# A coarser projection step and a swapped order of two preparation streams in a planned one-core mixer kernel

## Chip, core and metric

The kernel runs on one core of a Trainium2 chip. The metric is device time in microseconds, the median of several executions. TensorE is called PE, VectorE DVE, ScalarE ACT, GpSimd POOL; SP issues most transfers. PE's clock has two levels, 2.4 GHz (1.0 in the profile's column of granted clock) and 1.2 GHz (0.5).

## What is computed

One layer over 640 tokens (128 of context, 512 latent) of width 1024. A normed and modulated input `h` is projected once to 8832 columns; two branches use them and are merged.

```
z = h @ w_in                                   # r,k,v,decay,iclr | gate A | q,k,v | gate B | merge gates
branch A: per head and direction, a scan over the tokens:
    sa = s @ a_t ;  s = s * w_t + sa b_t^T + v_t k_t^T ;  y_t = s @ r_t
branch B: windowed attention with cached context keys and a sink
out = x + gate * ((sig(m_a) * (yA*silu(g_a)) @ w_oA + sig(m_b) * (yB*silu(g_b)) @ w_oB) @ w_out)
```

## The kernel before, in words

All products with big weights are float32 made of three float32r products: weight high by input high, weight low by input high, weight high by input low (tiles `wh`, `wl` by `hh`, `hl`). A block of 128 columns is two halves of 320 tokens, a half is 8 slices (`k`) of 1024 inputs, so 24 products of 320 columns into one PSUM tile `g`. The generator `products` runs through the blocks. It also loads the weights (`wr`, three buffers, over SP), splits them (ACT makes `wh`, POOL makes `wl`) and lets the evacuation (`late`) of the half before come behind slices 0 and 2.

The scan of branch A is done in chunks of 64 tokens for 8 pairs of heads. Each pair passes through five streams, and each stream is a generator that stops wherever something has to become ready:

- `fronts`: key norm, decay and rate gates by a small product (`mi<-dw`, `mi<-da`, evacuated by ACT into `cs` and `ta`), the scaled operands `ar` and `bk`, the chunk matrices (four groups of 10 products `mi<-ar,bk 64x64`, each evacuated by DVE into `XT`), and the bonus (`mi<-rk`, evacuated by DVE into `rk`).
- `backs`: inversion of those matrices. DVE first inverts 16 by 16 corners (14 rounds of `X<-M`, `M<-M,X` between two transposes); then PE and ACT go through six stages of 32 by 32 products for each of two halves, from `mi<-ident,X` to `mi<-XT,X`.
- `all_items`: score matrices and transposed operands (`sc<-ar,bk`, `sc<-ident,rkv`, `sc<-ident,bk`).
- `chains`: the scan itself, 10 steps for each pair, one after the other. A step is `ur<-St` on PE, `U` on DVE, `st<-U,XT` on PE, `SB` on ACT, `st<-SB` on PE, the new state `St` on DVE.
- `finishes`: group norm of the result on DVE, its transposes (`sc<-ident,ytok`).

The order on PE, ACT, DVE and POOL is written by `deal`. It keeps an estimated time for each engine (`Clock`). Before each step of the projection it goes through the list of streams from the front, and the first one that may go on (its last results count as ready, its condition holds, DVE and ACT are not over 2 us behind) makes one step; then the list is gone through from the front again. When no stream may go on, the projection makes one step, up to its next `yield`. Engines execute in that order, so an instruction that is not ready holds up all that stands behind it on its engine. The projection consists of 3312 products in this part; when they are used up, what is left of the streams runs alone, with the 16 products of `gate_rows` (`g<-wg`) strewn in by the scheduler. Small PSUM tiles `mi` have two buffers and `sc` one, so the third group of `mi` waits for the evacuation of the first. After `deal` comes the attention, then the output products.

Of the kernel before, what the change touches and what calls it, by code (L numbers as in the profile page):

```python
# [170 lines left out]
def hybrid_step(ctx, tc, a):  # L171
# [12 lines left out]
    def T(shape, tag, bufs, dt=F32, name=None):  # L184
        bufs = NB.get(tag, bufs)
        return sb.tile(shape, dt, tag=tag, name=name or tag, bufs=bufs)

    def PG():
        return psp.tile([P, 512], F32, tag="g", name="g", bufs=2)
# [193 lines left out]
    def products(blocks):  # L383


        blocks = iter(blocks)
        todo, raws = [], []
        over = [False]

        def more_raw():  # L390
            while len(raws) < 3 and not over[0]:
                if not todo or todo[-1][1] == 2:
                    b = next(blocks, END)
                    if b is END:
                        over[0] = True
                    if b is END or b is None:
                        return
                    todo.append([b, 0, None, None])
                t = todo[-1]
                raw = T([P, 4, P], "wr", 3, name="wr")  # L400
                k = 4 * t[1]
                nc.sync.dma_start(out=raw, in_=t[0][0].rearrange("(k p) n -> p k n", p=P)[:, k:k + 4, t[0][1]:t[0][1] + P])
                t[1] += 1
                raws.append((t, k, raw))

        def split():
            if not raws:
                return
            t, k, raw = raws.pop(0)
            if k == 0:  # L410
                t[2] = T([P, KB, P], "wh", 2, F32R, name="wh")
                t[3] = T([P, KB, P], "wl", 2, F32R, name="wl")
            act.copy(out=t[2][:, k:k + 4], in_=raw)
            pool_e.tensor_tensor(out=t[3][:, k:k + 4], in0=raw, in1=t[2][:, k:k + 4].bitcast(F32), op=ALU.subtract)

        more_raw()
        late = None
        done = 0
        while not over[0] or todo:
            if not todo:  # L420
                yield IDLE
                more_raw()
                continue
            t = todo.pop(0)
            while any(r[0] is t for r in raws):
                split()
            if t[1] < 2:
                todo.insert(0, t)
                more_raw()
                todo.pop(0)  # L430
                while any(r[0] is t for r in raws):
                    split()
            more_raw()
            (w, c0, xh, xl, evac, more), _, wh, wl = t
            for half in range(2):
                ps = PG()
                o = ps[:, :HALF + more]
                s = slice(0, HALF + more) if half == 0 else slice(HALF - more, TOK)
                for k in range(KB):
                    pe.matmul(out=o, lhsT=wh[:, k, :], rhs=xh[k][:, s], start=(k == 0), stop=False)  # L440
                    pe.matmul(out=o, lhsT=wl[:, k, :], rhs=xh[k][:, s], start=False, stop=False)
                    pe.matmul(out=o, lhsT=wh[:, k, :], rhs=xl[k][:, s], start=False, stop=(k == KB - 1))
                    if k == 0 and late:
                        late = late[0](*late[1:])
                    if k == 2 and late:
                        late = late()
                    if k == 2:
                        split()
                        more_raw()
                    if k == KB - 1:  # L450
                        late = (evac, half, o, s)
                        if not todo and half == 1:
                            late = evac(half, o, s)
                            if late:
                                late()
                            late = None
                    yield None

    def gemm(*args, **kw):
        for _ in products([gemm_block(*args, **kw)]):  # L460
            pass
# [73 lines left out]
    def filler():  # L535

        for nm, col, nb, kind in (("kb", COL_KB, 2, "plain"), ("vb", COL_VB, 2, "plain"), ("q", COL_Q, 8, "plain"),
                                  ("ga", COL_GA, 8, "silu"),
                                  ("gb", COL_GB, 8, "silu"), ("ma", COL_MA, 8, "tanh"), ("mb", COL_MB, 8, "tanh")):
            for b in range(nb):  # L540
                spills[nm, b] = dram_.tile([P, TOK], F32, name="sp_%s%d" % (nm, b))
                yield spill(col + P * b, spills[nm, b], kind)
# [20 lines left out]
    for _ in products([conv_block(COL_WA, wa, 24)]):  # L563
        pass
# [15 lines left out]
    def project(i):  # L580

        us[i]["rkv"] = [dram_.tile([P, TOK], F32, name="sp_rkv%d%d" % (i, j)) for j in range(3)]
        return [conv_spill(c0 + P * i, us[i]["rkv"][j], 8 * j + i, i if j == 2 else None)
                for j, c0 in enumerate((COL_R, COL_K, COL_V))]
# [14 lines left out]
    def load(i):  # L599
        if i < NPAIR and us[i].get("projected") and "loaded" not in us[i]:  # L600
            us[i]["loaded"] = [T([P, TOK], "rkv", 4, name="rkv%d" % j) for j in range(3)]
            for t, d in zip(us[i]["loaded"], us[i]["rkv"]):
                nc.sync.dma_start(out=t, in_=d)
            us[i]["at"] = clock.at["pe"] + 5
# [857 lines left out]
    def plan():  # L1462

        fill = filler()
        nxt = 0
        while True:
            if nxt < NPAIR and (nxt < 2 or us[nxt - 2].get("begun")):
                yield from project(nxt)
                nxt += 1
                continue  # L1470
            b = next(fill, None)
            if b is None and nxt == NPAIR:
                return
            yield b

    def fronts():
        for i in range(NPAIR):
            yield lambda: us[i].get("projected")
            us[i]["begun"] = True
            load(i)  # L1480
            clock.run.ready = max(clock.run.ready, us[i]["at"])
            yield
            yield from front(i, us[i])

    def backs():
        for i in range(NPAIR):
            yield lambda: us[i].get("ready")
            yield from back(us[i])
            us[i]["prepared"] = True

    def all_items():
        for i in range(NPAIR):
            yield lambda: us[i].get("ready")
            for n in range(5):
                yield lambda: i == 0 or us[i - 1].get("step", 0) >= 2 * n + 2
                yield from items(us[i], n)
                us[i]["items"] = n + 1
            us[i]["itemized"] = True

    def chains():  # L1500
        for i in range(NPAIR):
            yield lambda: us[i].get("prepared") and us[i].get("items", 0) >= 1 and (i < 2 or us[i - 2].get("finished"))
            for x in chain(i, us[i]):
                yield x
                yield lambda: us[i]["items"] >= min(us[i]["step"] + 1, 9) // 2 + 1
            us[i]["chained"] = True

    def finishes():
        for i in range(NPAIR):
            yield lambda: us[i].get("chained")  # L1510
            yield from finish(i, us[i])
            us[i]["finished"] = True

    def deal(main, others):


        runs = [Run(o, clock) for o in others]
        more = True
        while more or any(r.steps for r in runs):
            went = True  # L1520
            while went:
                went = False
                for j, r in enumerate(runs):
                    if not r.open() or j and max(clock.at["dve"], clock.at["act"]) > clock.at["pe"] + BACKLOG:
                        continue
                    clock.run = r
                    r.step()
                    clock.run, went = None, True
                    break
            before = clock.at["pe"]  # L1530
            more = more and next(main, END) is not END
            if clock.at["pe"] == before:
                clock.at["pe"] += 0.1

    with tc.tile_pool(name="psc", bufs=1, space=PSUM) as pools["scan"], tc.manual_schedule(engines=ORDERED):
        deal(products(plan()), [chains(), finishes(), all_items(), backs(), fronts()])
    for _ in gate_rows():
        pass
    pools["ur"] = ctx.enter_context(tc.tile_pool(name="psu", bufs=1, space=PSUM))
# [87 lines left out]
```

## Time and profile before

| | us |
|---|---|
| median of 3 runs | 1523.27 |
| lowest, highest | 1522.05, 1525.69 |
| profiled execution | 1514.24 |
| its span (first to last instruction) | 1512.5 |

The profiled execution took 9.0 us less than the median of the runs. In the profile an fp32 product of the small kind is two records, a float32r product one. A bracket at the end of a line tells how long the engine had been idle before it and what ended that. "issue" stands where nothing that the profile shows was waited for.

### The profile page before, as it was taken

The page shows a single profiled execution, that of the slowest core. Times are in us where ns is not written, and L with a number is a line of the kernel's source. Part 1 is how long each engine was busy: PE and PEld are TensorE (multiplying, and loading weights), DVE is VectorE, ACT ScalarE, POOL GpSimd, SP SyncE. Part 2 cuts the span into 40 slices and gives each one's busy share as a digit, 9 for nine tenths or more (in the row PEclk, how much of TensorE's full clock was granted, in tenths as well). Part 3 has the DMA queues.
Part 4 walks back from the last instruction along what each step waited for, and adds up shares of the span by engine and source line. Part 5 has one row for each costly group of instructions (what it writes and reads, how often), then busy time and mean ns, then how long its engine had stood idle before and what let it go on. Part 6 is the DMA issues. An engine that isn't in the chain of part 4 may idle for free.

```text
span 1512.5 us, 40280 instructions
## 1 busy us (share of the span) xinstructions
PE 1326.8 (88%) x16959; PEld 1094.7 (72%) x16959; DVE 789.3 (52%) x1818; ACT 682.5 (45%) x1661; POOL 451.3 (30%) x476
## 2 busy tenths in 40 slices
PE   5699899989989989998999999999854589999996
PEld 0499788878878887787887887788443356668985
DVE  2437516804553582465357147236226898763636
ACT  2335264364346426534643652653433465654322
POOL 0323333323233322323223243242222222233630
PEclk9699899999999999999999999999965599999999
DMA  8143312322221232223122212223322242224532
GB/s 315 39 136 106 97 52 80 96 70 61 87 89 56 65 95 67 69 82 100 52 80 85 78 57 87 73 73 102 116 69 66 79 137 68 85 74 149 183 111 93
DMA packets 154419, 139.05 MB, mean 92 GB/s; under 512 B 16435, under 2 KB 130294, under 8 KB 154238
## 3 DMA queue, kind: packets, MB, share of 16 engines
q1 hardware_dynamic: 144328, 126.27, 26.9%
q10 hardware_dynamic: 9910, 10.21, 2.1%
q8 instruction: 133, 2.18, 0.6%
q14 instruction: 48, 0.39, 0.1%
HBM read 102.88 MB, written 33.56 MB: 90 GB/s over the span
## 4 chain that ended last, share of the span: by engine, by line
PE 67%; DVE 14%; ACT 7%; issue 5%; DMA 1%; POOL 1%; ACTq 0%; DVEq 0%; SPq 0%; POOLq 0%
PE g L139 38%; PE mi L139 10%; PE st L139 8%; PE sc L139 7%; PE ur L139 5%; DVE X L139 3%; DVE M L139 2%; ACT L139 1%; DVE ytok L139 1%; ACT X L139 1%; DVE St L139 1%; ACT SB L139 1%; DVE gnt L139 1%; DVE o L139 1%; DVE nm L139 1%
## 5 line engine op out<-in xcount | busy, mean ns | idle before, releaser
L139 POOL TENSOR_TENSOR wl<-wr,wh 128x512 fp32r<-128x512 f32 x170 | 230.3, 1357 | 694.9 <-ACT wh L139 658.0
L139 PE MATMUL g<-hh,wh 128*128 128x320 f32 (+1 forms) x1104 | 383.9, 348 | 9.8 <-DVE stg L139 4.9
L139 PE MATMUL g<-hl,wh 128*128 128x320 f32 (+1 forms) x1104 | 350.8, 318 | 1.5 <-POOL hl L139 1.2
L139 PE MATMUL g<-hh,wl 128*128 128x320 f32 (+1 forms) x1104 | 351.1, 318 | 0.8 <-issue 0.8
L139 PEld LDWEIGHTS g<-hh,wh 128*128 128x128 f32 x1104 | 215.2, 195 | 31.3 <-DVE stg L139 5.8
L139 PEld LDWEIGHTS g<-hh,wl 128*128 128x128 f32 x1104 | 216.8, 196 | 2.1 <-issue 1.1
L139 PEld LDWEIGHTS g<-hl,wh 128*128 128x128 f32 x1104 | 215.9, 196 | 3.0 <-POOL hl L139 2.2
L139 ACT CAST wh<-wr 128x512 fp32r<-128x512 f32 x170 | 104.5, 619 | 17.9 <-DMA wr<-in_w_oB 5.4
L139 ACT COPY SB<-st 64x128 f32<-64x128 f32 x160 | 41.8, 261 | 106.5 <-PE st L139 105.6
L139 ACT COPY U<-st 128x128 f32<-128x128 f32 x80 | 21.4, 267 | 145.1 <-DVE St L139 135.0
L139 DVE SCALAR_TENSOR_TENSOR stg<-g,vt,stg 128x127 f32<-128x127 f32 (+1 forms) x144 | 60.7, 436 | 38.3 <-ACT stg L139 35.6
L139 DVE SCALAR_TENSOR_TENSOR St<-St,pc,st 128x64 f32<-128x64 f32 x128 | 30.2, 276 | 93.5 <-PE st L139 85.3
L139 PE MATMUL mi<-ar,bk 64*64 64x64 f32 (+1 forms) x960 | 72.8, 247 | 6.3 <-DVE XT L139 6.0
L139 ACT COPY SB<-sc 64x256 f32<-64x256 f32 (+1 forms) x160 | 55.3, 372 | 47.8 <-PE sc L139 46.5
L139 DVE TENSOR_TENSOR S<-sc,smask 128x512 f32<-128x512 f32 x40 | 27.5, 687 | 90.8 <-PE mi L139 89.3
L139 POOL TENSOR_TENSOR S<-S,smask 128x512 f32<-128x512 f32 x40 | 49.1, 1227 | 79.9 <-ACT S L139 79.2
L139 DVE TENSOR_TENSOR U<-ur,U 128x128 f32<-128x128 f32 x72 | 20.8, 289 | 93.2 <-PE ur L139 90.2
L139 PEld LDWEIGHTS mi<-ar,bk 64*64 64x64 f32 (+1 forms) x960 | 62.2, 156 | 8.7 <-issue 4.5
L139 ACT ACTIVATE Pl<-ur,nm 128x384 f32<-128x384 f32 (+1 forms) x64 | 40.6, 636 | 34.5 <-DVE nm L139 27.6
L139 PE MATMUL ur<-KH,qt 128*128 128x512 f32 (+2 forms) x80 | 34.4, 434 | 22.7 <-ACT Pc L139 10.0
L139 ACT COPY X<-mi 32x320 f32<-32x320 f32 (+5 forms) x120 | 35.8, 330 | 39.0 <-PE mi L139 38.4
L139 ACT COPY PT<-sc 128x512 f32<-128x512 f32 x60 | 35.1, 585 | 39.9 <-PE sc L139 38.3
(284 smaller groups left out, 2934.2 us busy)
## 6 DMA issues: line engine op xcount, KB each, us to landing
wr<-in_w_in SPq DMA_DIRECT2D x138, 256.0 KB
sp_rkv<-stg SPq DMA_DIRECT2D x48, 160.0 KB
rkv<-sp_rkv SPq DMA_DIRECT2D x24, 320.0 KB
wa_t<-in_w_ada SPq DMA_DIRECT2D x11, 512.0 KB
wg<-in_w_ada SPq DMA_DIRECT2D x16, 256.0 KB
wr<-in_w_oA SPq DMA_DIRECT2D x16, 256.0 KB
wr<-in_w_oB SPq DMA_DIRECT2D x16, 256.0 KB
wo<-in_w_out SPq DMA_DIRECT2D x16, 256.0 KB
```

Of the source, the lines that this page charges most:

```text
L139: return f(**kw)
```

## The change

A step of the projection now ends behind every second slice, so six products go out between two looks at the streams, where it was three. And `fronts` stands ahead of `backs` in the list.

```
                     late = None
-                    yield None
+                    if k % 2:
+                        yield None
...
-        deal(products(plan()), [chains(), finishes(), all_items(), backs(), fronts()])
+        deal(products(plan()), [chains(), finishes(), all_items(), fronts(), backs()])
```

Neither line adds or removes arithmetic; they move instructions on every engine between the first front and the last chain. From the last `sc<-ident,ytok` on, the order on PE, ACT, DVE and POOL is the same in both.

First place, PE, the chunk matrices of the seventh pair (`mi<-ar,bk 64x64`, 40 products in four groups) among the steps of the chain of the pair before. Before:

```order
L139 MATMUL g<-hl,wh 128x320
L139 MATMUL mi<-ar,bk 64x64 x30
L139 MATMUL ur<-St_375,ar 64x64 x8
L139 MATMUL mi<-ar,bk 64x64 x10
L139 MATMUL g<-hh,wh 128x320
L139 MATMUL g<-hh,wl 128x320
L139 MATMUL g<-hl,wh 128x320
L139 MATMUL st<-U,XT 64x64 x4
```

Now:

```order
L139 MATMUL g<-hl,wh 128x320
L139 MATMUL st<-U,XT 64x64 x4
L139 MATMUL mi<-ar,bk 64x64 x20
L139 MATMUL st<-SB 64x64 x4
L139 MATMUL ur<-SB,S 64x64 x4
L139 MATMUL st<-SB,S 64x64 x4
L139 MATMUL mi<-ar,bk 64x64 x20
L139 MATMUL g<-hh,wh 128x320
```

The third group stood directly behind the second; now twelve products of the chain stand between the second and the third.

Second place, DVE, the last pair: the corner inversion (`M`, `X`), the bonus (`rk`), and the group norm of the pair before (`mu`). Before:

```order
L139 STREAM_TRANSPOSE M<-DG 128x1024
L139 SCALAR_TENSOR_TENSOR St_375<-St_375,pc,st 128x64 x2
L139 TENSOR_TENSOR ytok<-ur,ytok 64x128 x2
L139 TENSOR_TENSOR rk<-mi,rkv_11804 128x320 x2
L139 TENSOR_REDUCE mu<-ytok 128x10
L139 TENSOR_SCALAR mu<-mu 128x10
L139 TENSOR_TENSOR ytok<-ytok,mu 128x640
L139 TENSOR_TENSOR X<-M 128x28
L139 TENSOR_TENSOR M<-M,X 128x2x14
```

Now:

```order
L139 TENSOR_TENSOR rk<-mi,rkv_11633 128x320
L139 STREAM_TRANSPOSE M<-DG 128x1024
L139 SCALAR_TENSOR_TENSOR St_375<-St_375,pc,st 128x64 x2
L139 TENSOR_TENSOR ytok<-ur,ytok 64x128 x2
L139 TENSOR_TENSOR rk<-mi,rkv_11633 128x320
L139 TENSOR_TENSOR U<-ur,U 128x128
L139 TENSOR_TENSOR X<-M 128x28
L139 TENSOR_TENSOR M<-M,X 128x2x14
```

The group norm of pair seven stood ahead of and within the corner inversion of pair eight; it now stands behind it. The first half of the bonus has moved ahead of the transpose.

Third place, PE, the end of the projection (the last `g<-hl,wh`). Before, the first stage of the last inversion (`mi<-ident,X`) stands six rows behind the last row here:

```order
L139 MATMUL sc<-ar,bk 128x128
L139 MATMUL mi<-ar,bk 128x128
L139 MATMUL g<-wg,csil 2x512 x7
L139 MATMUL sc<-ident,ytok 128x128 x4
L139 MATMUL mi<-ident,ytok 128x128
L139 MATMUL g<-wg,csil 2x512
L139 MATMUL sc<-ident,rkv_11804 64x128
```

Now, right behind the last `g<-hl,wh`, and the first stage of the inversion itself:

```order
L139 MATMUL st<-U,XT 64x64 x4
L139 MATMUL g<-wg,csil 2x512
L139 MATMUL st<-SB 64x64 x4
L139 MATMUL ur<-SB,S 64x64 x4
L139 MATMUL st<-SB,S 64x64 x4
L139 MATMUL sc<-ar,bk 128x128
L139 MATMUL mi<-ar,bk 128x128
```

```order
L139 MATMUL mi<-ar,bk 128x128
L139 MATMUL mi<-ident,X 32x32 x40
L139 MATMUL ur<-St_375,ar 64x64 x8
L139 MATMUL mi<-ident,X 32x32 x40
L139 MATMUL st<-U,XT 64x64 x4
L139 MATMUL g<-wg,csil 2x512 x2
L139 MATMUL st<-SB 64x64 x4
```

The chain of the seventh pair used to be through when the projection ended; now its last two steps stand behind that end, among the first stage of the last inversion. Of the 16 `g<-wg`, 3 stood within the last chain before and 9 do now.

## Rows read from the trace of the kernel before

**Rows 1.** The page: span, and busy time of PE.

```profile
span 1512.5 us, 40280 instructions
PE 1326.8 (88%) x16959; PEld 1094.7 (72%) x16959; DVE 789.3 (52%) x1818; ACT 682.5 (45%) x1661; POOL 451.3 (30%) x476
```

**Rows 2.** Stretches: length, busy PE, PEld, DVE, ACT, POOL; last, granted clock, DMA share, GB/s.

```profile
130.00:1055.60 925.60, 864.34 (x13322) 748.44 (x13322) 463.14 (x1003) 440.67 (x1093) 295.99 (x340) 0.96 0.26 78
1055.60:1069.40 13.80, 11.06 (x54) 3.00 (x54) 12.49 (x42) 3.51 (x7) 3.06 (x4) 0.88 0.52 163
1069.40:1093.00 23.60, 18.61 (x797) 13.96 (x796) 1.38 (x2) 12.92 (x36) 4.42 (x9) 0.93 0.28 88
1093.00:1148.10 55.10, 33.49 (x520) 25.35 (x518) 11.52 (x40) 16.46 (x57) 9.35 (x12) 0.65 0.20 60
1148.10:1200.00 51.90, 20.76 (x68) 12.12 (x67) 45.83 (x98) 21.15 (x55) 17.85 (x11) 0.50 0.25 72
```

**Rows 3.** Waits of PE, 130 to 1055.6 us: us in total, times, longest.

```profile
PE mi L139 <- ACT cs L139: 9.8, 11, 2.0
PE mi L139 <- issue: 9.3, 7, 2.4
PE mi L139 <- DVE rk L139: 6.6, 4, 4.3
PE mi L139 <- DVE XT L139: 6.0, 6, 1.8
PE mi L139 <- ACT X L139: 5.8, 12, 2.1
PE g L139 <- DVE stg L139: 4.9, 2, 3.9
PE mi L139 <- DVE X L139: 3.9, 2, 3.5
PE mi L139 <- ACT XT L139: 3.8, 5, 1.2
```

**Rows 4.** PE in order of time, a chain step between projection products: start, us, what.

```profile
988.52 0.31 PE L139 MATMUL g<-hh,wl 128*128 128x320 f32 x1
988.66 0.31 PE L139 MATMUL g<-hl,wh 128*128 128x320 f32 x1
988.90 0.46 PE L139 MATMUL ur<-St,ar 64*64 64x64 f32 x16
989.29 0.42 PE L139 MATMUL g<-hh,wh 128*128 128x320 f32 x1
989.55 0.31 PE L139 MATMUL g<-hh,wl 128*128 128x320 f32 x1
```

**Rows 5.** PE in order of time: three single waits.

```profile
313.40 0.25 PE L139 MATMUL mi<-M,X 32*32 32x32 f32 x5 [2.38 <-issue]
...
402.18 1.01 PE L139 MATMUL mi<-ar,bk 64*64 64x64 f32 x20 [1.76 <-DVE XT L139]
...
432.91 1.10 PE L139 MATMUL mi<-ident,X 32*32 32x32 f32 x80 [4.28 <-DVE rk L139]
```

**Rows 6.** Stretches of 5 us behind two waits; columns as in rows 2.

```profile
435.00:440.00 5.00, 5.00 (x105) 4.79 (x104) 2.19 (x8) 0.99 (x4) 0.00 (x0) 0.83 0.29 87
465.00:470.00 5.00, 4.78 (x18) 4.58 (x18) 1.29 (x2) 2.79 (x7) 0.63 (x2) 0.50 0.28 85
```

**Rows 7.** PE in order of time: last projection product, last inversion, last chain.

```profile
1055.23 0.31 PE L139 MATMUL g<-hl,wh 128*128 128x320 f32 x1
...
1069.38 1.58 PE L139 MATMUL mi<-ident,X 32*32 32x32 f32 x160
...
1093.04 0.45 PE L139 MATMUL st<-SB,S 64*64 64x64 f32 x8
```

**Rows 8.** In order of time: two gate products on PE, a wait of ACT.

```profile
1087.52 1.62 PE L139 MATMUL g<-wg,csil 128*2 128x512 f32 x4
...
1103.33 0.62 ACT L139 CAST wh<-wr 128x512 fp32r<-128x512 f32 x1 [2.78 <-DMA wr<-in_w_oA]
```

## The prediction

> **What bounds the kernel now.** I read the page first: PE is busy for 1326.8 of 1512.5 us [rows 1], so what the change can give must be time in which PE stands still or runs at half clock. The stretches say where that is [rows 2]. From 130 to 1055.6 us the projection runs with the streams woven into it: PE is busy for 864.34 of 925.60 us, 61.3 us idle, at a mean granted clock of 0.96. Then the projection is used up, and the rest has three parts that follow each other: 13.8 us until the last inversion starts, 23.6 us of inversion, 55.1 us of the last chain, where PE is busy for 33.49 us only and its clock is 0.65. The starts of the three are in [rows 7]. What follows the last chain is ordered alike in both kernels, and DVE carries its first 52 us (45.83 busy); I take it as unchanged. So two questions: how much do 61.3 us of waits and the slow clock behind them shrink, and how long is the bare end.
>
> The list of PE's waits [rows 3] tells what the 61.3 us are. Its eight rows are 50.1 us; the other 11.2 us are scattered. Three kinds matter. First, waits at the start of an inversion for DVE: `X` 3.9 and `rk` 6.6, together 10.5. Second, waits within the inversion, for ACT's copies `X` 5.8 and `XT` 3.8 and under "issue" 9.3, together 18.9. Third, waits for one of the two `mi` buffers: `XT` 6.0 (chunk matrices) and `cs` 9.8 (gates). Single ones are in [rows 5].
>
> **Part A, fewer changes between projection and streams.** In the order the projection is cut into 306 runs before and 275 now, 31 fewer. Within a run the products start 0.14 us apart; from the last one to `ur` it is 0.24, and behind `ur` the first product takes 0.26 until the next [rows 4]. So a run costs about 0.10 + 0.12 = 0.2 us more than its products, and 31 of them 6 us. Two groups of streams that now meet also change the shape of PE's work between them, so I take 5 us, with 0 and 6 as ends.
>
> The Trainium skill (TensorE: Matmul & The Clock Gate, Architectural detail) says that PE pulls the next weight load ahead of running products. By that alone a change of shape would cost nothing, A would be 0 and the time 5 us higher. The rows show 0.2 us for each run here.
>
> **Part B, the waits while the projection runs.** The arithmetic is the same, so what counts is how much PE work stands between an instruction and the one that uses its result. I read that from the two orders.
>
> Inversion: between its first and last stage lie 83 projection products in the mean of seven pairs before, and 134 now, because the front of the next pair is served first and a step is twice as big. At 0.14 us each [rows 4] that is 7 us more cover over six stages. The waits for `X` and `XT` are 0.6 us each in the mean (9.6 us in 17), so most of that should go. The "issue" waits stand in the middle of bursts of 32 by 32 products, as at 313.40 [rows 5]: a group that was under way stops for 2.38 us though nothing it reads is late. I take this for the instruction stream running dry; spread bursts drain it more slowly. Of 18.9 us I take 10, ends 3 and 17.
>
> The Trainium skill (Runtime: NRT & Kernel Launch, Instruction fetch mechanics) says that fetching instructions ahead is mostly hidden. By that the 9.3 us have another cause, which spacing need not touch, and the gain here would be about 6 instead of 10. The 9.3 us in the middle of groups speak against it in this kernel.
>
> Start of the inversion: from the last chunk matrices to `mi<-ident,X` there are 110 products before and 112 now, no more than before, but the bonus is now evacuated before the corner inversion begins, wholly or in half, and the group norm no longer stands ahead of it on DVE. The 4.28 us at 432.91 were a wait for just that evacuation [rows 5]. Of 10.5 us I take 6, ends 2 and 10.
>
> Chunk matrices: before, the third group stands directly behind the second at 12 of 16 places; now at 3, elsewhere products of the chain or the projection lie between. Of 6.0 us [rows 3] I take 3, ends 1 and 5.
>
> Gates: here it gets worse. The places where only one pair of gate products stands between a group and the earlier one whose `mi` buffer it takes are 16 before and 28 now. The waits for `cs`, 9.8 us [rows 3], come from the 16, 0.6 us each; 12 more would be 7. I take 5, ends 0 and 8.
>
> Sum of B: 10 + 6 + 3 - 5 = 14 us less. The 4.9 us for `stg` and the scattered 11.2 us I leave as they are.
>
> **Part C, the clock behind the waits.** PE falls to 1.2 GHz behind long waits: after the 4.28 us the next 5 us run at 0.83, and another stretch of 5 us, behind a wait, lies at 0.50 throughout with PE busy for 4.78 us [rows 6], a loss of up to 2.4 us. The mean clock of 0.96 over 925.6 us bounds all of that by 37 us [rows 2]. If the waits shrink by a quarter, so does the loss, if long and short ones shrink alike: 9 us. Since part of the slow time lies where PE waits anyway, I take 6, ends 0 and 15.
>
> **Part D, the bare end.** First part: before, 13.8 us pass until `mi<-ident,X`, with DVE busy for 12.49 of them [rows 2], for the corner inversion and the group norm. Now the corner inversion stands mostly ahead of the end of the projection, and PE has 25 products until then: 16 of the chain, 8 of the items, one of the gate rows. One bare chain step is 5.5 us (55.1 / 10) and this is over half of one: 3.5 us. That is 10.3 less. Second part: the inversion has the last chain step of the pair before between its stages, 2 more gate products and the group norm's transposes; 3 us more. Third part: the last chain carries 9 gate products instead of 3. Two of them (four records) take 1.62 us at most [rows 8], so 6 more are 3 to 5 us, and the fourth set of items moves in. Some lies in gaps in which PE waits anyway; 3 us more. ACT's wait of 2.78 us for a weight in that chain [rows 8] may go or be another; I take 1 off. Sum: 10.3 - 3 - 3 + 1 = 5 less, with 10 less and 5 more as ends.
>
> **Sum.** 5 + 14 + 6 + 5 = 30 us less than 1514.2, so 1484 for a profiled execution. The median of the runs before lies 9.0 us above the profiled one, so I set 1523.3 - 30 = 1493. With the favourable ends (A 6; B 17 + 10 + 5 = 32; C 15; D 10) it would be 63 less: 1460. With the poor ones (A 0; B 3 + 2 + 1 - 8 = -2; C 0; D -5) it would be 7 more.
>
> **Rivals.** *The waits only move.* DVE and ACT have the same work and hold it in order; if a front that goes first delays the chain's `U` and `St` by what it spares the inversion, B and C come to nothing and A and D remain: 1523 - 10 = 1513, or 1518 if D's parts cancel too. For it: the front's operations stand in the same queue on DVE as the chain's, and at 432.91 such a queue cost PE 4.28 us [rows 5]. Against it: waits for `U` and `St` are not among the large rows [rows 3], so the chain has slack.
>
> *Slower: the chain falls behind the projection.* With a step of six a chain operation that has just become ready waits for up to 0.84 us instead of 0.42. In the order the chain of the seventh pair is two steps short when the projection ends. If the last inversion can't start earlier, because DVE is still busy with it, then two bare steps (11 us) and the gate products (3.5 us) come on top of the end, and with only A against them the result is 1523 + 14.5 - 5 = 1533. It decides from the point where the last `mi<-ident,X` stands later than about 14 us behind the last projection product, as it does now. Against it: in the order only the 25 products of part D stand between the two, and on DVE the transpose that ends the corner inversion stands ahead of the state update that the first four of them lead to.
>
> **How the numbers follow.** My forecast (1460 to 1510) gets 0.65, waits that only move (1510 to 1524) 0.18, the chain behind 0.17. The range from 1464 to 1524 leaves out the last and the tip of the first. A measurement of this kernel tells 0.2% from no change, 3 us: faster 0.75 (forecast and half of the second), same 0.09, slower 0.16.
>
> **What would show it.** Right: PE's idle time while the projection runs falls from 61 us to about 45; the waits for `X`, `XT` and `rk` before products into `mi` fall to below half; those for `cs` rise; the mean clock rises above 0.96; the last projection product comes near 1030 us instead of 1055; `mi<-ident,X` of the last pair follows within 4 us, and the last chain is 3 us longer. Wrong: new rows of PE waiting for `U`, `St` or `rho`; the last projection product at 1050 us or later; more than 10 us from it to `mi<-ident,X`.

## The result, and the profile after

The changed kernel takes **1474.9 us** (median of 4 runs, 1472.0 to 1479.9), the kernel before 1524.5 us in the same comparison: a ratio of 0.9676, with a 95% interval of 0.9642 to 0.9711, so 49.6 us less. The profiled executions are 1514.24 and 1471.97 us, 42.3 us apart; the rest is that the profiled execution of before lies further below its median.

The page after: span, and busy time of PE (before: [rows 1]).

```profile
span 1470.2 us, 40278 instructions
PE 1307.1 (89%) x16959; PEld 1079.7 (73%) x16959; DVE 791.8 (54%) x1818; ACT 677.0 (46%) x1661; POOL 455.1 (31%) x476
```

The stretches after, cut at the same points of the program as [rows 2] and with the same columns.

```profile
130.00:1012.20 882.20, 837.57 (x13230) 728.47 (x13228) 461.68 (x1004) 434.43 (x1086) 297.35 (x339) 0.98 0.27 81
1012.20:1015.50 3.30, 3.30 (x51) 2.18 (x50) 3.06 (x8) 0.86 (x3) 0.00 (x0) 1.00 0.34 111
1015.50:1044.40 28.90, 23.58 (x837) 15.42 (x833) 9.39 (x31) 14.81 (x41) 6.17 (x9) 0.88 0.32 94
1044.40:1102.40 58.00, 38.75 (x556) 26.75 (x554) 12.16 (x41) 18.30 (x61) 10.67 (x13) 0.70 0.28 84
1102.40:1154.30 51.90, 20.69 (x67) 12.12 (x67) 45.91 (x98) 21.05 (x55) 17.94 (x11) 0.50 0.25 72
```

Nearly all of the gain lies in the first row: from 130 us to the last projection product it is 882.2 us instead of 925.6, 43.4 less. Of these, 16.6 us are idle time and 16.0 the slow clock (reckoned as below). The other 10.8 are PE's work, of which 4.4 us are no longer needed; the rest now lies in the bare end and ahead of 130 us. The three parts of the bare end were 13.8 + 23.6 + 55.1 = 92.5 us and are 3.3 + 28.9 + 58.0 = 90.2. What follows the last chain takes 367.8 us instead of 364.4.

PE's waits in the first row's stretch (us in total, times, longest; before: [rows 3]).

```profile
PE mi L139 <- DVE XT L139: 7.4, 7, 1.1
PE mi L139 <- issue: 5.3, 6, 1.8
PE mi L139 <- ACT cs L139: 5.1, 11, 1.2
PE g L139 <- DVE stg L139: 4.6, 5, 1.7
PE mi L139 <- ACT M L139: 3.7, 2, 2.9
PE mi L139 <- DVE ytok L139: 3.3, 1, 3.3
PE mi L139 <- ACT S L139: 2.9, 5, 1.3
PE mi L139 <- ACT X L139: 2.3, 4, 0.9
```

The waits for `rk` (6.6), for DVE's `X` (3.9) and for ACT's `XT` (3.8) are gone, and those for ACT's `X` fell from 5.8 to 2.3. Those for DVE's `XT` rose from 6.0 to 7.4, and `M`, `ytok` and `S` are new ahead of products into `mi`.

PE in order of time after: the last projection product, the last inversion, the last chain ([rows 7] before).

```profile
1011.92 0.31 PE L139 MATMUL g<-hl,wh 128*128 128x320 f32 x1
...
1015.57 0.89 PE L139 MATMUL mi<-ident,X 32*32 32x32 f32 x80
...
1044.45 0.45 PE L139 MATMUL st<-SB,S 64*64 64x64 f32 x8
```

**Where the 45.7 us went** (end of the last chain, 1148.1 before and 1102.4 after). PE's idle time up to there fell from 124.3 to 102.0 us, by 22.3. The time lost to the slow clock fell by 18.9: in each stretch of 5 us, one less the granted clock, times PE's busy time, adds up to 55.0 before and 36.1 after. What remains, busy time less that loss, is 968.8 and 964.4, so 4.4 us less for the same products. 22.3 + 18.9 + 4.4 is 45.6.

### The profile page after: what moved, and what is told of

It reads as the page before. It is cut to its first block, busy times and chain, and to the rows that moved or that the text cites. A ratio compares the mean times of both kernels' runs of the same rounds, so it can differ in the third digit from the quotient of the medians.

```text
span 1470.2 us, 40278 instructions
## 1 busy us (share of the span) xinstructions
PE 1307.1 (89%) x16959; PEld 1079.7 (73%) x16959; DVE 791.8 (54%) x1818; ACT 677.0 (46%) x1661; POOL 455.1 (31%) x476
## 4 chain that ended last, share of the span: by engine, by line
PE 64%; DVE 12%; issue 7%; ACT 6%; DMA 4%; POOL 2%; SPq 0%; DVEq 0%; ACTq 0%; POOLq 0%
PE g L139 34%; PE mi L139 10%; PE st L139 8%; PE sc L139 7%; PE ur L139 5%; DMA wr<-in_w_oB 1%; DMA wo<-in_w_out 1%; POOL wl L139 1%; DVE St L139 1%; DVE ytok L139 1%; DVE X L139 1%; ACT SB L139 1%; DVE o L139 1%; POOL wol L139 1%; ACT L139 1%
## 5 line engine op out<-in xcount | busy, mean ns | idle before, releaser
L139 PE MATMUL g<-hh,wh 128*128 128x320 f32 (+1 forms) x1104 | 376.4, 341 | 11.4 <-DVE stg L139 4.6
L139 PE MATMUL g<-hl,wh 128*128 128x320 f32 (+1 forms) x1104 | 346.6, 314 | 1.7 <-POOL hl L139 1.5
L139 PE MATMUL g<-hh,wl 128*128 128x320 f32 (+1 forms) x1104 | 346.4, 314 | 0.0
L139 PEld LDWEIGHTS g<-hh,wh 128*128 128x128 f32 x1104 | 211.4, 191 | 31.0 <-issue 6.5
L139 PEld LDWEIGHTS g<-hl,wh 128*128 128x128 f32 x1104 | 211.9, 192 | 3.2 <-POOL hl L139 2.5
L139 PEld LDWEIGHTS g<-hh,wl 128*128 128x128 f32 x1104 | 212.4, 192 | 2.4 <-issue 1.9
L139 DVE SCALAR_TENSOR_TENSOR St<-St,pc,st 128x64 f32<-128x64 f32 x128 | 30.2, 277 | 121.8 <-PE st L139 98.8
L139 PE MATMUL ur<-KH,qt 128*128 128x512 f32 (+2 forms) x80 | 35.1, 443 | 22.7 <-ACT Pc L139 10.1
L139 DVE TENSOR_REDUCE nm<-ur 128x1 f32<-128x384 f32 (+2 forms) x68 | 41.5, 623 | 19.5 <-PE ur L139 18.7
```

The costliest lines, as they stand in the source:

```text
L139: return f(**kw)
```

## The experiments

The table has all kernels but the two with added waits; the text behind it takes them one by one. "Idle" and "clock" are taken from 130 us to the last projection product: PE's idle time, and (1 - granted clock) times length over stretches of 5 us. "Runs" and "spread" (projection products between first and last stage of an inversion, mean of seven pairs) are read from the order, the rest from the profiles. In e3 the mean holds two pairs that reach or pass the end of the projection (60 and 0 products); the five ahead of them have 132 to 216. `ident,X` is the start of the last inversion. Ratios are to runs of the kernel before on the same chip (medians of 1515 to 1524 us).

| kernel | first served | step | runs | spread | idle | clock | `ident,X` | last product | end of last chain | median us |
|---|---|---|---|---|---|---|---|---|---|---|
| before | back | 3 | 306 | 83 | 61.3 | 34.1 | 1069 | 1055 | 1148 | 1524.5 |
| e2 | back | 6 | 271 | 65 | 72.4 | 46.1 | 1107 | 1033 | 1188 | 1555.4 |
| e9 | back | 1 | 352 | 76 | 63.0 | 32.5 | 1026 | 1099 | 1115 | 1491.6 (1 run) |
| e1 | front | 3 | 310 | 119 | 38.6 | 6.9 | 994 | 1033 | 1087 | 1455.1 |
| after | front | 6 | 275 | 134 | 44.7 | 15.4 | 1016 | 1012 | 1102 | 1474.9 |
| e3 | front | 12 | 188 | 122 | 42.7 | 20.5 | 1085 | 915 | 1170 | 1540.3 (1 run) |
| e7 | front | 1 | 348 | 105 | 63.7 | 34.2 | 970 | 1106 | 1068 | 1468.4 |
| e10 | front | 6, then 3 | 277 | 134 | 47.4 | 17.1 | 1013 | 1032 | 1101 | 1471.0 |
| e8 | front, group norm last | 3 | 323 | 115 | 45.2 | 20.6 | 995 | 1061 | 1087 | 1458.5 |
| e11 | front, limit 1.5 | 3 | 291 | 163 | 51.1 | 13.6 | 994 | 1045 | 1093 | 1466.5 |
| e12 | front, limit 1.6 | 3 | 311 | 147 | 47.0 | 10.3 | 971 | 1047 | 1082 | 1447.8 |
| e13 | back, then front | 3 | 299 | 92 | 59.8 | 32.4 | 1048 | 1045 | 1136 | 1502.6 |

**The two halves apart.** Run e1 has the order of the streams alone:

```
-        deal(products(plan()), [chains(), finishes(), all_items(), backs(), fronts()])
+        deal(products(plan()), [chains(), finishes(), all_items(), fronts(), backs()])
```

> Only the first half of the change: the front stream is served ahead of the back stream, a step of the projection stays three products. In the order an inversion is then spread over 119 projection products in the mean (83 before, 134 with both halves), the projection is cut into 310 runs (306 before, 275 with both), and both halves of the last inversion start ahead of the last projection product. Theory, that the gain comes from the spread: PE's idle time while the projection runs falls from 61.3 us to about 45 and the time lost to the slow clock from 34 us (0.037 x 925.6) to about 15, as with both halves; the switches cost 5 us more than with both; the bare end is shorter by the first part and the inversion, which are now paid in the projection. About 1475 us. Rival, that the step of six brings the gain: a mean clock of 0.96 and 60 us idle as before, about 1510 us.

Measured 1455.1 us, ratio 0.9565 (0.9534 to 0.9596): better than both lines together. Stretches of e1, the projection and the bare end:

```profile
130.00:1033.00 903.00, 864.41 (x14163) 744.55 (x14161) 472.73 (x1047) 455.76 (x1139) 296.03 (x351) 0.99 0.27 81
1033.00:1086.95 53.95, 38.52 (x535) 22.66 (x534) 11.96 (x40) 15.62 (x53) 10.52 (x13) 0.78 0.40 122
```

PE is idle for 38.6 us in the projection and the clock is 0.99. The last inversion is over when the projection ends, so only the chain is bare. So the swap brings the gain and not the step of six, as the theory had it; that it does so by the spread is not shown by this run. The time was 20 us too cautious: the theory expected the waits of the changed kernel, and there are fewer.

Run e2 has the step of six alone:

```
-                    yield None
+                    if k % 2:
+                        yield None
```

> Only the second half of the change: a step of six products, the back stream still ahead of the front stream. In the order an inversion is spread over 65 projection products (83 before), the projection is cut into 271 runs, and behind the last projection product 20 chain steps remain instead of 10. Theory, that the gain comes from the spread: idle time in the projection of 61 us or more and a clock loss of 34 us or more, 5 us less for fewer runs, and ten bare chain steps more at 5.5 us each, of which about 33 us of PE's work are taken out of the projection, 22 us on balance: about 1540 us. Rival, that the step of six brings the gain: idle and clock loss fall as with both halves, about 1500 us.

Measured 1555.4 us, ratio 1.0238 (1.0190 to 1.0287), slower than the kernel before. Stretches of e2: projection, the time until the last inversion, inversion, last chain.

```profile
130.00:1033.40 903.40, 831.03 (x12606) 725.74 (x12606) 428.68 (x923) 413.09 (x1016) 280.21 (x318) 0.95 0.25 77
1033.40:1106.60 73.20, 54.09 (x747) 35.96 (x745) 41.98 (x95) 28.99 (x81) 19.02 (x26) 0.79 0.35 104
1106.60:1129.90 23.30, 18.80 (x783) 15.41 (x783) 8.21 (x27) 14.56 (x39) 5.17 (x9) 0.79 0.17 54
1129.90:1188.40 58.50, 38.92 (x538) 30.81 (x536) 10.76 (x39) 15.00 (x54) 5.66 (x9) 0.53 0.07 18
```

The projection is used up 22 us earlier than before, but the last inversion starts 37 us later (1106.6 instead of 1069.4). So the two lines have opposite signs: the swap takes 64 us away (1519.3 to 1455.1), and the step of six gives back 36 us on the old order and 20 on the swapped one (1455.1 to 1474.9, medians of two comparisons; 17 by the ratios).

**The step, finer and coarser.** Run e7 has the swap and a `yield None` behind each of the three products, e9 the same without the swap, e3 the swap and a step of twelve (`if k % 4 == 3:`).

> The front stream ahead as in the change, but a step of the projection of one product instead of six (or three). In the order no chain step is left behind the last projection product (12 with the change, 9 with the swap alone), the projection is cut into 348 runs (275, 310) and an inversion is spread over 105 products (134, 119). Theory, that the step sets how closely the streams follow the projection: the bare chain of 54 us of the run with the swap alone goes into the projection, where it costs the 25 us or so that PE needs for it at full clock; 38 more runs at 0.2 us are 8 us, and the smaller spread brings 5 us of waits and clock back: about 16 us less than the swap alone, 1440 us. Rival, that spread alone counts: waits and clock as between before and the swap alone, no gain at the end, 1465 to 1475 us.

> A step of one product, the back stream ahead of the front stream as before the change. In the order 3 chain steps are left behind the last projection product (10 before), 352 runs (306), and an inversion is spread over 76 products (83). Theory, that spread sets waits and clock and the step sets the end: idle time of 61 us or more and a clock loss of 34 us or more in the projection, as before; the bare end shrinks from 92.5 us to about 25, of which some 40 us come back as PE's work in the projection; 46 more runs cost 9 us: about 1505 us. Rival, that a finer step also removes the waits: 1470 us or less.

> The change with a step of twelve products instead of six. In the order 188 runs (275), 30 chain steps behind the last projection product (12), and a spread of 122 products. Theory: 87 fewer runs at 0.2 us are 17 us less; 18 more bare chain steps at 5.5 us are 99 us more, of which PE's work of some 45 us is taken out of the projection; about 1510 us. Rival, that fewer switches are worth more than the bare end: below 1475 us.

Measured: e7 1468.4 us, ratio 0.9631 (0.9591 to 0.9670); e9 1491.6; e3 1540.3, the last two in one run each. e9 kept the waits of the kernel before (63.0 idle, 32.5 clock) and gained at the end, 16 us bare, as the theory had it; its time is 13 us below the theory's. The coarse side has the theory's direction and 30 us more than its price: e3's projection is over at 914.8 us and leaves 254.9 us bare, with PE busy for 189.47 of them.

```profile
130.00:914.80 784.80, 742.15 (x10767) 662.76 (x10767) 374.47 (x807) 355.97 (x874) 256.31 (x288) 0.97 0.28 84
914.80:1169.70 254.90, 189.47 (x3903) 143.11 (x3903) 110.29 (x280) 111.08 (x317) 49.23 (x73) 0.71 0.18 53
```

The fine side of the theory fails on the swapped order: e7 should have been better than e1 and is 13 us worse. Its last chain ends at 1068, 19 us ahead of e1's, but 38 us of projection are left over behind it, and on the way to it PE waits for 63.7 us and loses 34.2 to the clock. The time lies in the rival's range (1465 to 1475), but not for its reason: with a spread of 105, between 83 and 119, the rival had the waits between those of before and of e1, and they are as large as before. So spread alone does not set the waits. That a step of one leaves a stream's next instruction the least cover may be the cause; no run shows it.

**The step in its place.** Run e10 has a step of six until the front of the last pair has begun, and of three from then on (`if k % 2 or len(pools) and us[7].get("begun"):`).

> The front stream ahead, a step of six products until the front of the last pair has begun, of three from then on. In the order 277 runs, a spread of 134 products, both halves of the last inversion ahead of the last projection product, 10 chain steps behind it (12 with the change, 9 with the swap alone). Theory, that the step of six loses at the end alone, where the chain falls behind: the bare end is that of the swap alone (54 us, 5 more for one step), and 33 fewer runs give 5 to 10 us: about 1453 us. Rival, that it loses all along, by the 6 us of idle time and the 8.5 us of clock that the changed kernel has more in the projection than the swap alone: these stay, about 1465 us.

Measured 1471.0 us, ratio 0.9693 (0.9643 to 0.9742): the rival's side. Start of the last inversion in e10:

```profile
1013.35 0.89 PE L139 MATMUL mi<-ident,X 32*32 32x32 f32 x80
```

It stands at 1013.35 as with the change (1015.57), not at 993.8 as in e1, and the last chain ends at 1101.4 instead of 1102.4, though the projection lasts 20 us longer. So the lag of the streams behind the projection is built up over all pairs; a finer step at the end only spreads the same fill.

**The clock behind waits.** Runs e5 and e6 are the changed kernel with added waits, PE's order unchanged. In every eighth (e6: fourth) half block, ahead of slice 5, three (e6: one) times:

```
+    pool_e.engine.tensor_scalar(out=wl[:, 4:8], in0=wl[:, 4:8].bitcast(F32), scalar1=1.0,
+                                scalar2=None, op0=ALU.mult)
```

> The changed kernel with 17 added waits of PE, evenly spread over the projection: in every eighth half block POOL writes half of the low weight tile again with its own values, three times, and the next product waits for it. PE's order is that of the changed kernel. A POOL operation of that size takes 1.35 us where it subtracts; so a wait is about 3.8 us, 64 us in all. Theory of the clock: behind such a wait PE runs some microseconds at 1.2 GHz and loses 1 to 2.4 us more, so the time rises by 64 and 17 to 40 us, and the clock loss in the projection (15 us in the changed kernel) rises by that. Rival, that the clock does not follow these waits: the loss stays at 15 us, and the time rises by at most 64 us.

> As the run with 17 waits, but with 33 waits of one POOL operation each, in every fourth half block: about 1.1 us a wait, 36 us in all. Theory that the clock loss follows the idle time whatever its pieces: it rises in the same proportion to the added idle time as with the long waits. Rival, that short waits leave the clock at 2.4 GHz: the loss stays near 15 us, and the time rises by about 36 us at most, less what other waits shrink by.

Measured 1608.0 and 1577.6 us, one run each. The added operation took 1.66 us in the mean of e6, so the waits are longer than I expected, 5.3 and 2.3 us in the mean. The wait for it, and the projection's stretch, in e5:

```profile
PE g L139 <- POOL wl L445: 84.0, 16, 6.6
```

```profile
130.00:1148.00 1018.00, 891.00 (x13277) 772.92 (x13277) 465.40 (x1015) 437.77 (x1092) 374.30 (x390) 0.92 0.23 71
```

And in e6:

```profile
PE g L139 <- POOL wl L445: 70.7, 31, 5.0
```

```profile
130.00:1123.10 993.10, 883.10 (x13250) 762.12 (x13250) 465.58 (x1010) 436.45 (x1089) 348.85 (x371) 0.94 0.24 72
```

In e5 idle time rises from 44.7 to 127.0 us and the clock loss from 15.4 to 80.2: 0.79 us for each us of wait. In e6 it is 110.0 and 58.0, 0.65 us for each. This loss also counts slow time in which PE waits anyway; weighted by PE's busy time it is 0.57 and 0.58 us for each, the same proportion in both. Both rivals fall, though waits as short as the 1.1 us I had meant were not tried. The stretch became 135.8 us longer for 82.3 us of idle time in e5, and 110.9 for 65.3 in e6, so a wait of PE here costs about one and two thirds of itself.

**How far the swap reaches.** In e8 the group norm's stream is served last (`[chains(), all_items(), fronts(), backs(), finishes()]`); e11 and e12 are e1 with a limit on how far DVE and ACT may lie behind PE in the plan of 1.5 and 1.6 us (`BACKLOG = 2.0` before).

> A step of three products, the front stream ahead of the back stream, and the group norm's stream (finishes) served last of all. In the order 4 chain steps are left behind the last projection product (9 with the swap alone), 323 runs, a spread of 115 products. Theory: five chain steps fewer in the bare end, 27 us, which cost some 13 us in the projection; 13 more runs cost 3 us: about 11 us less than the swap alone, 1444 us. Rival, that a late group norm holds its buffers: new waits for ytok or yT in the projection, and no gain, 1455 us or more.

> The swap alone (step of three), and the plan lets the streams below the chain go on only while DVE and ACT are no more than 1.5 us behind PE in its own reckoning, instead of 2.0. In the order 291 runs (310 with the swap alone), an inversion spread over 163 products (119), 8 chain steps behind the last projection product (9). Theory, that spread lowers waits and clock loss: less than 38.6 us idle and no more clock loss than 7 us in the projection, 19 fewer runs give 4 us, one bare chain step less 3 us: about 1443 us. Rival, that the spread is used up at 119: waits as with the swap alone or more, since the front that is held back comes later; 1455 us or more.

> As the run with 1.5 us, but 1.6: in the order 311 runs, a spread of 147 products, 6 chain steps behind the last projection product. Theory: the three chain steps fewer than with the swap alone are worth 3 x 5.5 us less the 2.5 us each that they cost in the projection, 9 us, and the spread lowers waits a little: about 1444 us. Rival, that waits and clock do not follow the spread any more: 1455 us.

Measured: e8 1458.5 us, ratio 0.9573 (0.9544 to 0.9601); e11 1466.5, 0.9659 (0.9613 to 0.9706); e12 1447.8, 0.9536 (0.9485 to 0.9587). e8 ends its last chain with e1 (1086.6 and 1087.0), but what follows takes 373.3 us instead of 366.3, so there is no gain. About half of that is the last group norm, whose last step on DVE starts at 1099.13 us instead of 1095.31; the rest was not followed up. The time is the rival's, its reason is not: new waits for `ytok` or `yT` in the projection don't show. e11 has the widest spread of all, 163, and 51.1 us of idle time, more than e1: the rival holds, and among these kernels more spread than some 120 brings no more. e12 gains where the theory put it, in the bare end:

```profile
130.00:1047.80 917.80, 870.79 (x14366) 752.61 (x14368) 481.96 (x1056) 461.52 (x1164) 307.43 (x358) 0.99 0.26 80
1047.80:1082.10 34.30, 25.45 (x312) 11.44 (x312) 8.31 (x28) 8.29 (x26) 5.06 (x4) 0.88 0.56 163
```

Its waits did not shrink (47.0 idle). It has the lowest median of all, and its slowest run (1449.4) lies below e1's fastest (1453.4); but the intervals of the ratios overlap, so that it is faster than e1 is not shown.

**The swap in one half.** Run e13 is the kernel before with the swap in force from the fifth pair on.

```
+                ahead = us[4].get("begun")
-                for j, r in enumerate(runs):
+                for j, r in enumerate(runs[:3] + runs[:2:-1] if ahead else runs):
```

> The kernel before with the swap in one half only: the back stream is served first until the front of the fifth pair has begun, the front stream from then on; a step of three products throughout. In the order everything up to the 1830th projection product (of 3312) is as before; after it an inversion is spread over 99 to 117 products instead of 87 to 96, and behind the last product the last inversion follows after some 2 us instead of 7, with 12 chain steps (10). Theory, that the swap itself takes away waits and clock loss wherever it is in force: up to 580 us 34.7 us idle and 22.0 us of clock loss as before; from there to the last projection product 18.9 and 3.5 as with the swap alone, instead of 26.6 and 12.0; with a bare end some 5 us shorter about 1500 us. Rival, that the second half of the kernel before is quiet for other reasons and the swap's gain comes from the first half and the bare end of the swap alone: 26 us idle and 12 us of clock loss in the second half, 1515 us.

Measured 1502.6 us, ratio 0.9931 (0.9893 to 0.9970), 12.8 us less than the kernel before on that chip (1515.4). Stretches of e13 up to the 1830th projection product and on to the last, then those of the kernel before:

```profile
130.00:580.80 450.80, 414.07 (x6257) 362.29 (x6255) 233.70 (x502) 205.21 (x501) 145.29 (x164) 0.95 0.26 79
580.80:1045.30 464.50, 441.53 (x6984) 379.68 (x6986) 227.88 (x511) 232.80 (x586) 154.85 (x176) 0.98 0.26 78
```

```profile
130.00:579.80 449.80, 415.17 (x6255) 363.28 (x6253) 235.13 (x503) 205.72 (x503) 145.18 (x164) 0.95 0.26 79
579.80:1055.60 475.80, 449.17 (x7069) 385.16 (x7070) 228.00 (x500) 234.95 (x590) 150.81 (x176) 0.97 0.25 77
```

The first half is unchanged, as it should be. In the second, idle time is 23.0 us (26.6 before, 18.9 in e1) and the clock loss 10.2 (12.0 and 3.5). The theory's 1500 us and the rival's 1515 were reckoned from about 1520, so they stand for some 20 and 5 us of gain; the 12.8 us lie between them, though 1502.6 looks like the theory's. The mechanism came by a third: of the 16 us that the theory expected in that stretch the swap brought 5.4, and the bare end is 1.8 us shorter (90.7 instead of 92.5) where 5 were expected. The bigger part of e1's gain lies in its first half, where 34.7 us of idle time became 19.7 and 22.0 us of clock loss 3.4.

## Why the prediction was right, and where it was not

The sign, the place and the range were right; 30 us were forecast, and the profiled executions are 42.3, the medians 49.6 us apart. Of the signs named, idle time (44.7 us, about 45 named), the mean clock (0.98), the waits for `rk`, `X` and ACT's `XT`, and `ident,X` within 4 us came. The last product came at 1012 us instead of 1030, the waits for DVE's `XT` and `cs` went the other way than named (`XT` up, `cs` down), and of the signs of being wrong small ones showed: `rho` 0.4 us, and DVE's `U` 2.2 instead of 0.5. The 30 us are a sum with errors in both directions, so that it came within 20 us is in part luck.

- **Part A**, 0.2 us for a run, 5 us: right. Busy time less clock loss up to the last chain's end falls from 968.8 to 964.4 us. Over the eleven kernels of the table other than e7 (whose projection outlasts the chain) it lies within 5.4 us of a line with 0.20 us for each run (947.5 at 188 runs, 977.1 at 352). The Trainium skill's early weight loads (TensorE: Matmul & The Clock Gate, Architectural detail) do not make a change of work free here.
- **Part B**, 14 us: the sum was right (16.6), its pieces were not all. Inversion, its start and the gates, by the shape of the product that waited, first of the kernel before (columns: busy, mean ns, idle ahead of it and its releasers):

```profile
L139 PE MATMUL mi<-M,X 32*32 32x32 f32 x1120 | 14.6, 199 | 8.5 <-issue 8.5
L139 PE MATMUL mi<-ident,X 32*32 32x32 f32 x1120 | 13.2, 201 | 10.6 <-DVE rk L139 6.6 <-DVE X L139 3.9
L139 PE MATMUL mi<-da,lh 128*128 128x320 f32 x30 | 12.0, 401 | 8.4 <-ACT cs L139 8.4
L139 PE MATMUL mi<-dw,lh 128*128 128x320 f32 x30 | 11.7, 395 | 4.5 <-ACT XT L139 1.9 <-ACT cs L139 1.4 <-ACT X L139 1.2
```

and of the kernel after:

```profile
L139 PE MATMUL mi<-ident,X 32*32 32x32 f32 x1120 | 13.4, 198 | 2.9 <-issue 2.5 <-DVE rho L139 0.4
L139 PE MATMUL mi<-M,X 32*32 32x32 f32 x1120 | 12.1, 194 | 0.9 <-issue 0.8
L139 PE MATMUL mi<-da,lh 128*128 128x320 f32 x30 | 11.9, 399 | 5.2 <-ACT cs L139 5.1
L139 PE MATMUL mi<-dw,lh 128*128 128x320 f32 x30 | 11.0, 370 | 5.1 <-ACT M L139 2.9 <-ACT S L139 1.1 <-issue 0.7
```

  All products of 32 by 32 and the `mi<-ident` beside them waited for 25.9 us before and 7.7 after, 18 less where I had taken 10 + 6. The start was undersized: all 10.5 us went, not 6. The prediction also put waits for ACT's `X` and `XT` into the inversion that stood elsewhere: of their 9.6 us, 3.1 were waits of the next front's `mi<-dw` and 1.1 of its key norm, for a buffer. Two pieces had the wrong sign. The chunk matrices wait for 7.4 instead of 6.0 us (I took 3 off), and the gates' waits for `cs` fell from 9.8 to 5.1 us where I added 5: counting places with only one pair of products in between did not tell whether ACT is late there. Together these pieces are 21.5 us less; 4.9 came back at rows that I had left as they were or that are new (`ytok` 3.3, `M` 2.9 at `mi<-dw`). That the sum fits is luck.
- **Part C**, the clock, 6 us: this is the term that was mis-sized. The loss fell from 34.1 to 15.4 us in the projection, 19 less; weighted by PE's busy time, which is how the term enters the sum, it fell from 30.2 to 14.2, 16 less where I took 6, and just beyond my favourable end of 15. The step that failed is "if the waits shrink by a quarter, so does the loss": idle time shrank by 27%, the loss by 55% (in e1 by 37% and 80%). The loss behind a wait is no fixed share of the idle time. e5 and e6 show that added waits cost 0.65 to 0.79 us of clock for each us; among the kernels without added waits it is about 1 us for each us (from e1 to before, 27 for 23).
- **Part D**, 5 us: 2.3. Its first part came out as worked out (3.3 us, 3.5 forecast), the last chain too (58.0, 2.9 longer); the inversion took 5.3 us more instead of 3. The stretch behind the last chain, taken as unchanged, gave 3.4 us back.
- **The rivals.** "The waits only move" fell, since the sum of the waits fell by 16.6 us; the 4.9 us under part B are what did move. "The chain falls behind the projection" is real, but its price is seen only against e1. There the step of six lets the last inversion start 22 us later and leaves 90.2 us bare instead of 54, and costs 20 us in all. I had booked the bigger step as more cover for the inversion (134 products against 83); 119 of them come from the swap alone, and the rest bought nothing.
- **"issue"** fell from 10.1 to 7.1 us (with its rows at `g`); at `mi` it was 13.7 and 14.3 in e2 and e9, 5.8 in e1. The Trainium skill (Runtime: NRT & Kernel Launch, Instruction fetch mechanics) holds fetching mostly hidden. No run was made to test what these waits are, but the traces tell something of it. Count PE's records (products, weight loads, semaphore instructions) in order of start: in all fourteen kernels the 122 "issue" waits of over 0.3 us between 130 and 1120 us stand at multiples of 256 records from each other, give or take one. The 256 records up to such a wait, with the wait, took 1.7 to 6.1 us, where 128 projection products and their weight loads take an estimated 18 (at 0.14 us each, [rows 4]). This speaks for the prediction's reading, that the stream of instructions runs dry where small products use it up quickly, block by block; at these places fetching would then not be hidden. Not each quick block is followed by a wait, and which ones are stays open.

What stays open too is why waits in e7 and e11 do not follow the spread. Compared with e1, in e7 "issue" (10.5 us instead of 5.8 at `mi`), `M` (9.0 instead of 5.3) and `ytok` (6.3, no row in e1) grew, in e11 `cs` (11.8 instead of 4.9), `ytok` (6.7) and `S` (5.8 instead of 1.0). Open as well is why the late swap of e13 brought a third of what e1 saves in the same stretch.

## What to carry to other kernels

Where a plan weaves dependent streams into a filler, look at when the last stream and the filler end: a coarse step let the filler run out here (255 us bare in e3), on the swapped order the finest left 38 us of it over (e7), and the best kernels lie between. Test the lines of a change apart, since a good one can carry a bad one. When you price a wait of PE, price the slow clock behind it as well.

## What was not expected of the hardware

A short wait among small products can be followed by the lower clock level, and the same wait elsewhere is not. In the kernel after, the fourth group of chunk matrices waited for 1.14 us:

```profile
254.94 1.26 PE L139 MATMUL mi<-ar,bk 64*64 64x64 f32 x20 [1.14 <-DVE XT L139]
```

```profile
250.00:255.00 5.00, 3.86 (x99) 3.42 (x99) 2.97 (x9) 1.03 (x5) 1.56 (x2) 1.00 0.48 142
255.00:260.00 5.00, 5.00 (x47) 4.43 (x48) 0.88 (x3) 0.17 (x1) 0.00 (x0) 0.51 0.00 0
260.00:265.00 5.00, 5.00 (x53) 4.04 (x53) 1.27 (x4) 1.62 (x6) 0.00 (x0) 0.81 0.11 36
```

Right behind it PE is busy without a gap, at 1.2 GHz for 5 us and partly for the next 5: some 3.4 us (0.49 x 5 + 0.19 x 5) for a wait of 1.14. In the same kernel a wait as long ahead of another pair's chunk matrices, behind the same products of the chain, left the clock at 1.00:

```profile
374.61 1.38 PE L139 MATMUL mi<-ar,bk 64*64 64x64 f32 x40 [1.14 <-DVE XT L139]
```

```profile
375.00:380.00 5.00, 5.00 (x78) 4.22 (x75) 1.18 (x3) 1.00 (x3) 1.52 (x2) 1.00 0.19 56
```

So did a wait of 3.26 us for `ytok` that ended at 809.87 us (1.00 from 805 to 820). The length of a single wait does not tell what it costs; the prices above are means over many waits.
